# Moving tiles at drawn positions modulo 256 bytes in a two-layer decoder trunk

## The chip, the cores and the metric

One core of one Trainium2 chip runs the kernel. The metric is the device time in microseconds of one execution, as the median of several runs.

## The reference

Two layers on 256 tokens of width 2048, fp32. Each layer has a token mixer and then a gated network with a causal convolution of width 3; each of these four parts is preceded by an RMS norm with a shift and scale that come from a conditioning vector, and followed by a gate. Cut to what matters here:

```python
def stick_breaking_mixer(h, qkv_w, o_w):
    ...
    o = stick_breaking_attention(qkv[0], qkv[1], qkv[2])
    o = o.transpose(0, 2, 1, 3).reshape(bsz, t_len, d)
    return o @ o_w                              # 2048 -> 2048

def conv_ffn(h, up_w, dw_w, dw_b, down_w):
    u = causal_depthwise_conv(h @ up_w, dw_w, dw_b)      # 2048 -> 2 x 5632
    gt, val = jnp.split(u, 2, axis=-1)
    return (jax.nn.silu(gt) * val) @ down_w              # 5632 -> 2048

# layer 0: convolution module, conv_ffn; layer 1: stick_breaking_mixer, conv_ffn; final norm
x = x + gate * y
x = x + gate * conv_ffn(h, ffn_up_w[i], ffn_dw_w[i], ffn_dw_b[i], ffn_down_w[i])
```

## The kernel before

Everything is held transposed: a tile has 128 features on the partitions and the 256 tokens along the row. A product of two fp32 matrices is made of three matmuls in the type fp32r, since each operand is split into a high part (rounded) and a low part (the rest). The weights are the stationary operand, `wh` and `wl`; the activations are the moving operand, a pair of tiles of 256 columns. The function `gemm` writes them at lines 298 to 300 of the kernel (L298: high weights by high activations; L299: high weights by low activations; L300: low weights by high activations).

The moving pairs are:

- `hh`, `hl`: the normed input of a part, 16 pairs. They feed the first products of the networks ("up") and the products for queries and keys. They are not touched.
- `gh`, `gl`: the gated values between the two products of a network. A network's 44 tiles of 128 features go in two halves of 22; each half is made by an up product (`up_done` splits it into a pair) and consumed by a second product ("down"), which adds 22 tiles into each of the 16 output blocks. There are 23 buffers for the pairs, gh0 to gh22, so the second half begins with gh22, then gh0, gh1 and so on. The pool of network 0 is called g0, of network 1 g1.
- `oh`, `ol`: the results of the 16 attention heads, which feed the product "o".
- `zh`, `zl`: the output of the convolution module's norm, which feeds "pw2". Not touched.

The order of the matmuls comes from `plan`: the first four output blocks of a second product or of o take turns, tile by tile (four triples of matmuls on one moving pair, then the next pair); for the last four tiles, and for all the later blocks, one block runs over all its tiles. Down in halves is therefore 16 x 22 x 3 = 1056 matmuls, four such stages in the program; o is 16 x 16 x 3 = 768.

Weights arrive by DMA from SP's queue in pieces of 128 x 1024 (`raw`), ACT rounds them to `wh` (L244), and DVE makes `wl` (L248). During the network of layer 0, the rows for the later shifts, scales and gates come by DMA from POOL's queue into a ring of tiles `mraw` (three in one pool, two in a pool "mods" opened behind g0), and DVE reduces each (L331), in order between its other work.

Where a tile lies in its row of SBUF follows from the order in which a pool hands out tiles. The helper `skewed` allocates each of the z, g and o tiles 8 floats longer than its 256, so that the next tile begins 1056 bytes on, which is 32 bytes further modulo 256. The first tile of g0, of g1 and of o begins at 160 modulo 256:

```python
SKEW = {"z": (1, 1), "g0": (1, 1), "g1": (1, 1), "o": (1, 1)}
...
return pool.tile([P, T + 8 * SKEW[kind][low]], F32R, name=name)[:, :T]
...
gh[j] = skewed(gpool, f"g{i}", 0, f"gh{j % NG}")
gl[j] = skewed(gpool, f"g{i}", 1, f"gl{j % NG}")
```

High and low tiles alternate, so gh0, gl0, gh1, gl1 lie at 160, 192, 224, 0 and so on. The `hh` and `hl` tiles (258 floats, laid out in steps of 1056 bytes) have the same even steps.

Of the kernel before, what the change touches and what calls it, by code (L numbers as in the profile page):

```python
# [11 lines left out]
F32R = mybir.dt.float32r  # L12
# [4 lines left out]
P = 128  # L17
# [7 lines left out]
LATE_POOL, LATE_PE = 10, 8  # L25
PRODUCTS = 11

SKEW = {"z": (1, 1), "g0": (1, 1), "g1": (1, 1), "o": (1, 1)}
HEAD = 16
UBUFS = 9  # L30
M0 = 6
# [86 lines left out]
def hybrid_trunk(ctx: ExitStack, tc: tile.TileContext, cfg: Cfg, io: dict):  # L118
    nc = tc.nc
    D, T, H = cfg.D, cfg.T, cfg.H  # L120
# [115 lines left out]
    def split_next(later=False):  # L236

        blocks, v, n = raws[len(parts)]
        if stream[len(parts)][0] == "pw1":
            parts.append((blocks, v, None))  # L240
            return
        wh = w_pool.tile([P, PW], F32R, name="wh")
        wl = w_pool.tile([P, PW], F32R, name="wl")
        nc.scalar.copy(wh[:, :n], v[:, :n])  # L244
        parts.append((blocks, wh, wl))

        def low():
            nc.vector.tensor_tensor(wl[:, :n], v[:, :n], wh[:, :n].bitcast(F32), op=ALU.subtract)  # L248

        if later:  # L250
            return low
        low()
# [117 lines left out]

    def skewed(pool, kind, low, name):

        return pool.tile([P, T + 8 * SKEW[kind][low]], F32R, name=name)[:, :T]

    def split_act(t, hh, hl, bias=None):

# [119 lines left out]
    with ExitStack() as cv:  # L496
# [321 lines left out]
        for c in range(KD + 1):  # L818
# [6 lines left out]
            if c > 0:  # L825
                old = [(c - 1, k) for k in vector_taps(c - 1)[split(c - 1):]]
                n = max(len(taps), len(old))
                pad = lambda v: v + [None] * (n - len(v))
                taps = [t for pair in zip(pad(taps), pad(old)) for t in pair if t]
            made = 0  # L830
            for s in range(nd):
# [10 lines left out]
                if c == 0 and s % 2 == 1 and 2 + s // 2 < NH:  # L842
                    j = 2 + s // 2
# [5 lines left out]
                if c == KD and s == 0:  # L849
                    low = split_next(later=True)  # L850
# [68 lines left out]
        for j in range(KD + 1):  # L919
            if j < KD:  # L920
                zt.append(t256())
                if j > 1:
                    nc.vector.tensor_tensor(ys[j], ys[j], dm, op=ALU.subtract)
                nc.vector.tensor_tensor(zt[j], ys[j], rs, op=ALU.mult)
                nc.scalar.activation(zt[j], zt[j], AF.Silu, bias=pc("ln_b", j, 1), scale=pc("ln_g", j, 1))
            if j == 1:
                low()
            if j > 0:
                zs.append([skewed(zpool, "z", n == "zl", f"{n}{j - 1}") for n in ("zh", "zl")])
                split_act(zt[j - 1], *zs[j - 1])  # L930
            if j in (1, 2, 4):
                split_next()
# [18 lines left out]
    def ffn(i, entry, out):  # L951
        m = f"ffn{i}"
        NG = KF // 2 + 1
        with ExitStack() as fs:
# [16 lines left out]
            def up_done(nb, ps):  # L971
                pend[nb] = conv3(ps, nb)
                j = nb % KF
                if not (j in pend and j + KF in pend):
                    return
                yg, yv = pend.pop(j), pend.pop(j + KF)
                s = t256()
                nc.scalar.activation(s, yg, AF.Silu)
                nc.vector.tensor_tensor(s, s, yv, op=ALU.mult)
                gh[j] = skewed(gpool, f"g{i}", 0, f"gh{j % NG}")  # L980
                gl[j] = skewed(gpool, f"g{i}", 1, f"gl{j % NG}")
                nc.scalar.copy(gh[j], s)
                nc.vector.tensor_tensor(gl[j], s, gh[j].bitcast(F32), op=ALU.subtract)
# [57 lines left out]
    with ExitStack() as at:  # L1041
# [100 lines left out]
        for g in range(H // GH):  # L1142
            if g == 0:
                hh, hl = entry1.product("qk0a", qk_done, "natural_log_exp_and_others")
# [161 lines left out]
```

## Time and profile before

| | |
|---|---|
| median of 3 runs (range) | 2307.48 us (2307.41 to 2308.37) |
| span of the profiled execution, first to last instruction | 2304.7 us (the page gives no other time of it) |
| PE busy | 2270.8 us, 99% |
| DVE, ACT, POOL busy | 75%, 51%, 15% |
| HBM read | 598.58 MB, 261 GB/s over the span |
| granted TensorE clock, mean | 0.997 of full speed |

PE is TensorE's matmuls, PEld its weight loads, DVE VectorE, ACT ScalarE, POOL GpSimd, SP the engine whose queue issues most DMAs. The matmuls of one stream overlap: a matmul's own duration is longer than the distance from its start to the start of the next, and it is the distance that adds up. "PEclk" is the granted clock as a share of full speed (in tenths in the page's row of 40 slices).

In the profile the stages that use the touched tiles lie at: down of network 0, 668.0 to 792.1 us and 1027.4 to 1155.3; o, 1455.2 to 1547.8; down of network 1, 1808.2 to 1932.2 and 2167.6 to 2291.4.

### The profile page before, as it was taken

The page shows a single profiled execution, that of the slowest core. Times are in us where ns is not written, and L with a number is a line of the kernel's source. Part 1 is how long each engine was busy: PE and PEld are TensorE (multiplying, and loading weights), DVE is VectorE, ACT ScalarE, POOL GpSimd, SP SyncE. Part 2 cuts the span into 40 slices and gives each one's busy share as a digit, 9 for nine tenths or more (in the row PEclk, how much of TensorE's full clock was granted, in tenths as well). Part 3 has the DMA queues.
Part 4 walks back from the last instruction along what each step waited for, and adds up shares of the span by engine and source line. Part 5 has one row for each costly group of instructions (what it writes and reads, how often), then busy time and mean ns, then how long its engine had stood idle before and what let it go on. Part 6 is the DMA issues. An engine that isn't in the chain of part 4 may idle for free.

```text
span 2304.7 us, 44243 instructions
## 1 busy us (share of the span) xinstructions
PE 2270.8 (99%) x17834; PEld 2168.1 (94%) x17834; DVE 1736.7 (75%) x2386; ACT 1164.4 (51%) x1776; POOL 334.6 (15%) x478
## 2 busy tenths in 40 slices
PE   7999999999999999999999999999999999999997
PEld 5888678999999999999999999999999999999997
DVE  7689968899998899999975555668666545666654
ACT  2056655755543355554465555657555434555443
POOL 4058713200000000002111000121000000000010
PEclk9999999999999999999999999999999999999999
DMA  9988799789999999999854555555555555555553
GB/s 397 417 328 306 272 368 355 272 320 356 358 347 384 363 345 361 355 350 345 304 189 159 165 173 167 172 190 179 190 187 189 187 188 186 190 189 187 190 185 110
DMA packets 139167, 603.56 MB, mean 262 GB/s; under 512 B 15441, under 2 KB 15569, under 8 KB 115153
## 3 DMA queue, kind: packets, MB, share of 16 engines
q1 hardware_dynamic: 120242, 464.42, 56.0%
q0 software_dynamic: 18720, 136.32, 15.8%
q8 instruction: 139, 2.28, 0.4%
q14 instruction: 66, 0.54, 0.1%
HBM read 598.58 MB, written 2.10 MB: 261 GB/s over the span
## 4 chain that ended last, share of the span: by engine, by line
PE 88%; DVE 5%; DMA 4%; ACT 1%; issue 1%; POOL 0%; DVEq 0%; SPq 0%; POOLq 0%; ACTq 0%
PE ps L298 25%; PE ps L299 25%; PE ps L300 25%; PE ps L664 5%; DMA mraw<-in_mt_mix 3%; DVE mraw L331 2%; DVE wl L248 1%; PE ps L1133 1%; PE ps L1131 1%; PE ps L1132 1%; DMA mraw<-in_mt_ffn 1%; PE ps L577 1%; PE auxa L577 1%; DVE hl L382 0%; PE auxb L1132 0%
## 5 line engine op out<-in xcount | busy, mean ns | idle before, releaser
L248 DVE TENSOR_TENSOR wl<-raw,wh 128x1024 fp32r<-128x1024 f32 x688 | 842.9, 1229 | 412.7 <-ACT wh L244 408.0
L244 ACT CAST wh<-raw 128x1024 fp32r<-128x1024 f32 x688 | 719.5, 1048 | 823.9 <-PE ps L299 642.1
L298 PE MATMUL ps<-hh,wh 128*128 128x256 f32 (+1 forms) x3264 | 915.8, 281 | 0.0
L299 PE MATMUL ps<-hl,wh 128*128 128x256 f32 (+1 forms) x3264 | 912.1, 279 | 0.0
L300 PE MATMUL ps<-hh,wl 128*128 128x256 f32 (+1 forms) x3264 | 908.3, 278 | 0.1
L299 PEld LDWEIGHTS ps<-hl,wh 128*128 128x128 f32 x3264 | 617.7, 189 | 0.3
L300 PEld LDWEIGHTS ps<-hh,wl 128*128 128x128 f32 x3264 | 612.8, 188 | 0.7 <-DVE wl L248 0.7
L298 PEld LDWEIGHTS ps<-hh,wh 128*128 128x128 f32 x3264 | 612.7, 188 | 0.3
L299 PE MATMUL ps<-gl,wh 128*128 128x256 f32 x1408 | 396.0, 281 | 0.0
L300 PE MATMUL ps<-gh,wl 128*128 128x256 f32 x1408 | 393.7, 280 | 2.1 <-DVE wl L248 2.1
L298 PE MATMUL ps<-gh,wh 128*128 128x256 f32 x1408 | 394.9, 280 | 0.0
L331 DVE CUSTOM_DVE_ANT_0 mraw<-mraw,csr 128x2048 f32<-128x2048 f32 x152 | 348.2, 2292 | 46.3 <-DMA mraw<-in_mt_mix 30.2
L300 PEld LDWEIGHTS ps<-gh,wl 128*128 128x128 f32 x1408 | 265.5, 189 | 2.3 <-DVE wl L248 2.3
L299 PEld LDWEIGHTS ps<-gl,wh 128*128 128x128 f32 x1408 | 266.5, 189 | 0.0
L298 PEld LDWEIGHTS ps<-gh,wh 128*128 128x128 f32 x1408 | 265.6, 189 | 0.0
L397 POOL TENSOR_TENSOR sumsq<-sumsq,t 128x256 f32<-128x256 f32 x56 | 66.2, 1183 | 879.8 <-ACT t L393 879.5
L664 PE MATMUL ps<-hh,raw 128*128 128x256 f32 x832 | 188.8, 382 | 0.0
L664 PEld LDWEIGHTS ps<-hh,raw 128*128 128x128 f32 x832 | 157.8, 191 | 28.3 <-issue 5.8
L967 DVE SCALAR_TENSOR_TENSOR t<-ps,par,t 128x254 f32<-128x254 f32 x328 | 157.3, 480 | 3.9
L704 DVE SCALAR_TENSOR_TENSOR auxb<-u,cpar,auxb 128x256 f32<-128x256 f32 x297 | 121.6, 483 | 4.5 <-ACT auxb L688 3.7
L839 POOL TENSOR_TENSOR y<-y,hl 128x256 f32<-128x256 f32 x143 | 104.4, 730 | 13.4 <-ACT hl L713 3.3
L964 ACT ACTIVATE t<-ps,par 128x256 f32<-128x256 f32 x164 | 91.9, 560 | 0.0
(247 smaller groups left out, 2270.5 us busy)
## 6 DMA issues: line engine op xcount, KB each, us to landing
raw<-in_w_down SPq DMA_DIRECT2D x176, 512.0 KB, 4.5
mraw<-in_mt_ffn POOLq DMA_DIRECT2D x64, 1024.0 KB, 8.3
raw<-in_w_pw SPq DMA_DIRECT2D x96, 512.0 KB, 8.0
mraw<-in_mt_mix POOLq DMA_DIRECT2D x48, 1024.0 KB, 8.2
raw<-in_w_up01b SPq DMA_DIRECT2D x84, 512.0 KB, 7.0
raw<-in_w_up11b SPq DMA_DIRECT2D x84, 512.0 KB, 3.5
raw<-in_w_up00b SPq DMA_DIRECT2D x80, 512.0 KB, 7.6
raw<-in_w_up10b SPq DMA_DIRECT2D x80, 512.0 KB, 3.5
```

The source lines that it names most:

```text
L244: nc.scalar.copy(wh[:, :n], v[:, :n])
L248: nc.vector.tensor_tensor(wl[:, :n], v[:, :n], wh[:, :n].bitcast(F32), op=ALU.subtract)
L298: nc.tensor.matmul(o, wh[:, c], xh[kt], start=first, stop=False, skip_group_check=halves > 0)
L299: nc.tensor.matmul(o, wh[:, c], xl[kt], start=False, stop=False, skip_group_check=halves > 0)
L300: nc.tensor.matmul(o, wl[:, c], xh[kt], start=False, stop=left[nb] == 0, skip_group_check=halves > 0)
L331: nc.vector.tensor_tensor_reduce(out=v, in0=v, in1=csr, scale=1.0, scalar=0.0, op0=ALU.mult, op1=ALU.add, accum_out=macc[:, nb:nb + 1])
L397: engine.tensor_tensor(self.sum, self.sum, sq, op=ALU.add)
L664: nc.tensor.matmul(banks[j][:, nb // KD * T:(nb // KD + 1) * T], w[:, b * P:(b + 1) * P], hf[kt], start=first, stop=left[j] == 0, skip_gro ...
L704: nc.vector.scalar_tensor_tensor(conv_ps[j], us[j % UBUFS][:, k:k + T], tap(j, k), conv_ps[j], op0=ALU.mult, op1=ALU.add)
L839: nc.gpsimd.tensor_tensor(ys[c], ys[c], pr, op=ALU.add)
L964: nc.scalar.activation(y, ps[:, :T], AF.Identity, bias=pc(f"fdb{i}", nb, 1), scale=w(FW - 1))
L967: nc.vector.scalar_tensor_tensor(y[:, s:], ps[:, :T - s], w(k), y[:, s:], op0=ALU.mult, op1=ALU.add)
```

## The change

The even steps of g0, g1 and o are replaced by a table. For each name a position modulo 256 bytes, in steps of 32, is taken from a shuffled list of the 64 pairs (position of the high tile, position of the low tile), with a fixed seed for each pool; the tiles are padded in front and behind so that they land there. In g1 every position has 16 bytes more (the argument `half`). z keeps its even steps. Nothing else changes: the same instructions stand in the same order on every engine.

```diff
-SKEW = {"z": (1, 1), "g0": (1, 1), "g1": (1, 1), "o": (1, 1)}
+def phases(names, base, half, seed):
+
+    rng = np.random.default_rng(seed)
+    n = len(names) // 2
+    pairs = [(a, b) for a in range(8) for b in range(8)]
+    rng.shuffle(pairs)
+    want = [p for pair in pairs[:n] for p in pair]
+    out, at = {}, base
+    for i, name in enumerate(names):
+        pad = (want[i] - at // 32) % 8 if i == 0 else 0
+        nxt = 0 if i + 1 == len(names) else (want[i + 1] - (at // 32 + pad + 32 + half)) % 8
+        size = (pad + 32 + half + nxt) * 8
+        out[name] = (pad * 8 + 4 * half, size)
+        at += size * 4
+    return out
+
+
+G_NAMES = [f"g{x}{j}" for j in range(23) for x in "hl"]
+O_NAMES = [f"o{x}{j}" for j in range(16) for x in "hl"]
+PHASES = {"g0": phases(G_NAMES, 160, 0, 1), "g1": phases(G_NAMES, 160, 1, 2), "o": phases(O_NAMES, 160, 0, 3)}
...
     def skewed(pool, kind, low, name):
 
-        return pool.tile([P, T + 8 * SKEW[kind][low]], F32R, name=name)[:, :T]
+        if kind == "z":
+            return pool.tile([P, T + 8], F32R, name=name)[:, :T]
+        at, n = PHASES[kind][name]
+        return pool.tile([P, n], F32R, name=name)[:, at:at + T]
```

The positions that come out, in units of 32 bytes modulo 256, for the first pairs (high, low): before, in all three pools, (5,6) (7,0) (1,2) (3,4) (5,6) (7,0); after, g0 (7,5) (3,0) (4,5) (3,1) (7,2) (3,6); g1 (5.5,6.5) (3.5,3.5) (3.5,4.5) (3.5,1.5) (7.5,1.5) (5.5,4.5); o (5,4) (0,0) (0,4) (0,2) (3,7) (0,3).

## The prediction

> **What bounds the kernel now.** I read the page first: the busy time by engine, and the chain of work that ended last by line.
>
> ```profile
> span 2304.7 us, 44243 instructions
> PE 2270.8 (99%) x17834; PEld 2168.1 (94%) x17834; DVE 1736.7 (75%) x2386; ACT 1164.4 (51%) x1776; POOL 334.6 (15%) x478
> PEclk9999999999999999999999999999999999999999
> PE 88%; DVE 5%; DMA 4%; ACT 1%; issue 1%; POOL 0%; DVEq 0%; SPq 0%; POOLq 0%; ACTq 0%
> ```
>
> TensorE is busy for 99% of the span at its full granted clock, and 88% of the chain is PE. A nanosecond more per matmul is a nanosecond more of span wherever PE never waits. Next come the groups of PE by form; the change touches the rows with gh, gl, oh and ol.
>
> ```profile
> L298 PE MATMUL ps<-hh,wh 128*128 128x256 f32 x3072 | 861.0, 280 | 0.0
> L299 PE MATMUL ps<-hl,wh 128*128 128x256 f32 x3072 | 857.8, 279 | 0.0
> L300 PE MATMUL ps<-hh,wl 128*128 128x256 f32 x3072 | 853.8, 278 | 0.0
> L299 PE MATMUL ps<-gl,wh 128*128 128x256 f32 x1408 | 396.0, 281 | 0.0
> L298 PE MATMUL ps<-gh,wh 128*128 128x256 f32 x1408 | 394.9, 280 | 0.0
> L300 PE MATMUL ps<-gh,wl 128*128 128x256 f32 x1408 | 393.7, 280 | 2.1 <-DVE wl L248 2.1
> L298 PE MATMUL ps<-oh,wh 128*128 128x256 f32 x256 | 71.8, 281 | 0.0
> L299 PE MATMUL ps<-ol,wh 128*128 128x256 f32 x256 | 71.6, 280 | 0.0
> L300 PE MATMUL ps<-oh,wl 128*128 128x256 f32 x256 | 71.2, 278 | 0.0
> ```
>
> So 4224 matmuls read gh and gl, and 768 read oh and ol: 4992 whose moving address moves. The durations overlap, so they are no cost. The cost is the distance from one start to the next, which I take from stretches of known count: one output block over 22 moving tiles is 66 matmuls, over 16 tiles 48. (A stretch's x also counts the two or three matmuls that overlap its ends, so I use the plan's count.)
>
> ```profile
> core 0: us, PE busy (x), PEclk, DMA share, GB/s
> 668.03:693.57 25.54, 25.54 (x219) 1.00 0.96 369
> 699.18:703.08 3.90, 3.90 (x36) 1.00 1.03 385
> 703.08:706.93 3.85, 3.85 (x35) 1.00 0.99 388
> 803.42:809.02 5.60, 5.60 (x51) 1.00 0.80 309
> 1560.31:1568.96 8.65, 8.65 (x75) 1.00 0.20 61
> 1480.72:1542.32 61.60, 61.60 (x531) 1.00 0.58 189
> ```
>
> PE never idles in these and the clock is full, yet the pace differs:
> - 803.42 to 809.02, one block of the up product over the 16 hh/hl pairs: 5.60 us / 48 = 116.67 ns. Along the tiles the position climbs evenly (hh, hl 32 B on, back to hh, next hh 64 B on), and 16 steps of 64 B close the circle of 256 B, so the pattern never breaks.
> - 1480.72 to 1542.32, eleven blocks over the 16 oh/ol pairs, with the same steps: 61.60 / 528 = 116.67 ns.
> - 699.18 to 703.08, the first 33 matmuls of a block of the second product: 3.90 / 33 = 118.2 ns. Its 22 tiles end at position 224 (gh21) and begin again at 160 (gh0), a jump that breaks the pattern.
> - 703.08 to 706.93, the other 33 of the same block: 3.85 / 33 = 116.7 ns, back at the even pace.
> - 668.03 to 693.57, the opening of that product, where four blocks take turns so that a tile is read four times before the next: 25.54 / 216 = 118.2 ns.
> - 1560.31 to 1568.96, the 258-wide form of the up product, four blocks in turn: 8.65 / 72 = 120.1 ns; less two columns at 116.67/256 each it is 119.2 ns.
>
> DMA traffic does not set this: it is as high in the slow half as in the fast half of one block (385 and 388 GB/s). I read it so: the order of positions modulo 256 B sets the pace, an even order runs at 116.67 ns, and one break costs about 47 ns over the next 33 matmuls before the even pace returns.
>
> **The change part by part.** No instruction is added, removed or moved: on every engine and queue, SP's and POOL's too, the same instructions stand in the same order with the same waits. What differs is addresses. Writes of gh, gl, oh, ol by ACT and DVE keep their size; both engines have slack (51% and 75%). The pools grow by some 4 KB, which shifts the two extra ring tiles of the modulation rows and the attention's small tiles; the nearest rows for a matmul at other positions give at most 3 ns (120.1 against 116.67), and fewer than 300 attention matmuls make that under 1 us either way: taken as nothing.
>
> The matmuls are the term. In the drawn order hardly a step is the old one: gh0, gl0, gh1, gl1, gh2, gl2 lie at 224, 160, 96, 0, 128, 160 bytes modulo 256 in the first network. The pattern is broken at every tile and does not get its 33 matmuls to settle. The lower end for a matmul is the even pace, 116.67 ns; the upper end is 119.2 ns (the disturbed 258-wide form). The nearest rows are the 118.2 ns behind one break and in the opening; as breaks now follow each other without pause I go a little above, to 118.6 ns. The stages as they stand:
>
> ```profile
> 668.03:792.10 124.07, 124.07 (x1057) 1.00 0.98 378
> 1027.42:1155.27 127.85, 125.71 (x1057) 0.99 0.86 322
> 1808.16:1932.23 124.07, 124.07 (x1057) 1.00 0.57 187
> 2167.55:2291.44 123.89, 123.89 (x1057) 1.00 0.47 154
> ```
>
> Each has 1056 matmuls: 1056 x 118.6 = 125.24 us. Against 124.07 that is +1.17 us, twice; against 123.89, +1.35, twice (the second stage, with its stall taken out, is built like the fourth). Together +5.0 us. The heads' product has 576 matmuls behind its opening, from 116.67 to 118.6 ns: +1.1 us, and its opening of 192 at about 118.2 adds 0.1. Sum +6.2 us.
>
> One cover takes something back. In the second stage PE stalls, and the chain there shows why:
>
> ```profile
> 1050.98 2.20 DVE mraw L331
> ...
> 1088.66 7.93 DMA mraw<-in_mt_ffn
> 1096.65 2.18 issue
> ...
> 1100.49 0.38 PE ps L300
> ```
>
> Between 1051 and 1100.5 us the end is set by the modulation rows (a load that DVE waits for, in order, ahead of the weights' low parts), not by PE. Some 400 matmuls lie in there, and 1.2 ns more on each, 0.5 us, vanishes in the stall. How the stall is built:
>
> ```profile
> DVE mraw L331 <- DMA mraw<-in_mt_ffn: 5.5, 2, 5.2
> PE ps L300 <- DVE wl L248: 2.1, 1, 2.1
> 1101.00:1105.00 4.00, 4.00 (x23) 0.57 0.85 309
> ```
>
> PE waits 2.1 us, and then runs four microseconds at a granted clock of 0.57, which costs 1.7 more. If the shorter wait kept the clock up, 1.7 us would come back; if the load landed later, the same could be lost. The wait would still be 1.6 us, near the 2.1 that we see, so I take nothing. The stall goes on being set by DVE and DMA; nothing new becomes late elsewhere, since every engine that feeds PE gets more time.
>
> Sum: +6.2 - 0.5 = +5.7 us. The profiled span of 2304.7 becomes 2310.4. The page gives no time of its own beside the span; the median of the timed runs, 2307.48, lies 2.8 above it, so I forecast 2313.2 us, +0.25%. Below 0.2% (4.6 us) this measurement can't tell a change from none.
>
> [...]
>
> **The rivals.**
> - No change that can be told. The pace has only two levels in these rows, and drawn steps may be as often good as bad: DVE, clock and width all equal, a block now averages 7.75/66 = 117.4 ns, half disturbed and half not. If drawn positions average the same 117.4, the networks give 0 and the heads' product 576 x 0.75 = +0.4 us; at 118.2 it is +3.4 + 0.9 - 0.3. That gives 2307.5 to 2311.5 us. For it: 118.2 is what two of the disturbed rows show. Against: those rows still have even stretches in them.
> - Faster. What decides is the pace of the drawn order: to be told from no change it must be below 116.5 ns (4.6 us / 4992 = 0.92 ns under the present mean of 117.4). At 116.2 ns the stages lose 1.36 us twice and 1.18 twice, the heads' product 0.3: -5.4 us, 2302.1 us. For it: each block now loses 47 ns to its break, and a drawn order might happen not to fall behind. Against: no stretch that I read runs below 116.67 ns over a whole block.
> - Slower by more, through the second network's start at an odd 16 bytes: its tiles would touch a piece more at the end. The row nearest is the 258-wide form, 8 bytes past a full tile: 120.14 - 116.67 = 3.5 ns, of which two columns are 0.9. The other 2.6 ns on 2112 matmuls is 5.4 us on top: 2318.6 us. Against: part of the 2.6 belongs to the taking of turns.
>
> **How the numbers follow.** Forecast (about 118.6 ns) 0.45; odd 16 bytes 0.13, slower too; no change that can be told 0.34; faster 0.08. Slower is therefore 0.58, same 0.34, faster 0.08. The ends of the matmul term give 2304.4 (all at 116.67: -0.87 twice, -0.69 twice) and 2316.2 us (all at 119.2); with the odd 16 bytes 2318.6. The range leaves out the part under 2308 and over 2319 us.
>
> **What would show it.** In the profile after: the stretch of one block of the second product (66 matmuls) at about 7.83 us instead of 7.75, with no fast second half; a stage of 1056 at 125.2 us; the up products' blocks still at 5.60 us; a block of the heads' product at 5.69 instead of 5.60. If the second network's stages are longer than the first's by more than 1 us, the odd 16 bytes cost. I am wrong if the blocks stand at 7.75 us or below, or if the stall near 1100 us changes by more than the matmuls do.

## The result and the profile after

The changed kernel takes 2312.48 us (median of 18 runs), the kernel before beside it 2308.12 us: +4.4 us, ratio 1.0019 with a 95% interval of 1.0012 to 1.0026. The interval is clear of 1, so it is slower, by a little less than the 0.2% (4.6 us) that the prediction named as the least that can be told from no change.

The first lines of the page after:

```profile
span 2309.9 us, 44243 instructions
PE 2275.9 (99%) x17834; PEld 2173.0 (94%) x17834; DVE 1736.5 (75%) x2386; ACT 1164.9 (50%) x1776; POOL 333.3 (14%) x478
PE 87%; DVE 6%; DMA 4%; issue 1%; ACT 1%; POOL 0%; DVEq 0%; SPq 0%; POOLq 0%; ACTq 0%
```

The span is 5.2 us longer and PE's busy time 5.1 us longer; DVE and ACT work as long as before (1736.7 and 1164.4 us). The longer part is TensorE itself. The groups of PE by form show which matmuls (columns: count, busy us, mean ns of one, idle before):

```profile
L317 PE MATMUL ps<-hh,wh 128*128 128x256 f32 x3072 | 861.0, 280 | 0.0
...
L317 PE MATMUL ps<-gh,wh 128*128 128x256 f32 x1408 | 396.3, 281 | 0.0
L319 PE MATMUL ps<-gh,wl 128*128 128x256 f32 x1408 | 396.1, 281 | 2.3 <-DVE wl L267 2.2
L318 PE MATMUL ps<-gl,wh 128*128 128x256 f32 x1408 | 395.6, 281 | 0.0
...
L317 PE MATMUL ps<-oh,wh 128*128 128x256 f32 x256 | 72.3, 283 | 0.0
```

The hh group is the same to the tenth (861.0 us). The two gh groups and the oh group grew, the gl group did not (396.0 before): these are sums of durations that overlap (280 ns each where starts lie 118 ns apart), so they only point at the place. The distance between starts is again read from stretches of known count. First the kernel before, ten whole blocks of the second product of network 0 (660 matmuls), of o (480), and of the two halves of network 1 (660 each):

```profile
core 0: us, PE busy (x), PEclk, DMA share, GB/s
706.93:784.47 77.54, 77.54 (x663) 1.00 0.99 379
1486.32:1542.32 56.00, 56.00 (x483) 1.00 0.58 189
1847.06:1924.60 77.54, 77.54 (x663) 1.00 0.58 186
2206.41:2283.81 77.40, 77.40 (x662) 1.00 0.46 152
```

and the changed kernel, with ten blocks of the up product (480) ahead of them:

```profile
810.01:866.01 56.00, 56.00 (x482) 1.00 0.91 342
707.41:785.41 78.00, 78.00 (x662) 1.00 0.99 373
1488.70:1545.56 56.86, 56.86 (x482) 1.00 0.55 186
1850.57:1928.77 78.20, 78.20 (x662) 1.00 0.54 183
2210.89:2288.96 78.07, 78.07 (x663) 1.00 0.44 150
```

The untouched up product stands at 56.00 / 480 = 116.67 ns, as before. Network 0 goes from 117.5 to 78.00 / 660 = 118.18 ns, o from 116.67 to 56.86 / 480 = 118.46, network 1 from 117.5 and 117.3 to 118.48 and 118.29 ns. The clock is full and PE never idle in all of them. The fast second half of a block is gone: by the start times in the trace, averaged over eleven blocks of network 0, the first 33 matmuls of a block start 118.0 ns apart and the other 33 118.4 (before, 118.2 and 116.8). The whole stages after:

```profile
668.40:793.10 124.70, 124.70 (x1058) 1.00 0.99 376
1028.41:1157.36 128.95, 126.61 (x1057) 0.99 0.85 319
1457.42:1551.13 93.71, 93.71 (x789) 1.00 0.54 180
1811.49:1936.47 124.98, 124.98 (x1057) 1.00 0.56 186
2171.81:2296.64 124.83, 124.83 (x1057) 1.00 0.45 152
```

```profile
1455.21:1547.80 92.59, 92.59 (x789) 1.00 0.56 183
```

Against the prediction's rows of before, and this one for o, the five stages are longer by 0.63, 1.10, 1.12, 0.91 and 0.94 us: 4.7 of the 5.2 us. Another 0.4 lies ahead of 668 us, where no touched tile has been read (the stage begins at 668.40 instead of 668.03). In the experiments that leave the weights in place it begins anywhere from 668.2 us (e7) to 669.5 (e10), so this part is not put down to the change.

### The profile page after: what moved, and what is told of

Its sections match the earlier page's. It is cut to its first block, busy times and chain, and to the rows that moved or that the text cites. A ratio compares the mean times of both kernels' runs of the same rounds, so it can differ in the third digit from the quotient of the medians.

```text
span 2309.9 us, 44243 instructions
## 1 busy us (share of the span) xinstructions
PE 2275.9 (99%) x17834; PEld 2173.0 (94%) x17834; DVE 1736.5 (75%) x2386; ACT 1164.9 (50%) x1776; POOL 333.3 (14%) x478
## 4 chain that ended last, share of the span: by engine, by line
PE 87%; DVE 6%; DMA 4%; issue 1%; ACT 1%; POOL 0%; DVEq 0%; SPq 0%; POOLq 0%; ACTq 0%
PE ps L317 25%; PE ps L318 25%; PE ps L319 25%; PE ps L686 5%; DMA mraw<-in_mt_mix 3%; DVE mraw L350 2%; DMA mraw<-in_mt_ffn 1%; DVE wl L267 1%; PE ps L1153 1%; PE ps L1155 1%; PE ps L1154 1%; PE ps L599 1%; PE auxa L599 1%; DVE hl L404 0%; PE auxb L1154 0%
## 5 line engine op out<-in xcount | busy, mean ns | idle before, releaser
L419 POOL TENSOR_TENSOR sumsq<-sumsq,t 128x256 f32<-128x256 f32 x56 | 64.8, 1158 | 886.2 <-ACT t L415 886.0
```

Source lines behind the costliest of these rows:

```text
L419: engine.tensor_tensor(self.sum, self.sum, sq, op=ALU.add)
```

## The experiments

The question was what in a position costs time. The theory of the prediction, "breaks": any even order of positions settles at 116.67 ns, and what costs is a break in it. Rivals: each order has a pace of its own; the odd 16 bytes of the second network; and what is not an order of the moving tiles at all, their position against the weights, which all lie at 32 modulo 256. (Positions are worked out from the order of allocation; the profile shows no addresses.) All kernels use one helper in place of the table, and differ in the wanted positions (units of 32 bytes):

```diff
+def placed(names, base, want):
+    out, at = {}, base
+    for name, w in zip(names, want):
+        pad = int(w * 32 - at) % 256
+        size = -(-(pad + 1024) // 32) * 32
+        out[name] = (pad // 4, size // 4)
+        at += size
+    return out
+def even(n, first, low, step):
+    return [(first + step * j + i * low) % 8 for j in range(n) for i in range(2)]
+def drawn(n, seed, half=0):
+    pairs = [(a, b) for a in range(8) for b in range(8)]
+    np.random.default_rng(seed).shuffle(pairs)
+    return [p + half / 2 for pair in pairs[:n] for p in pair]
```

`even(23, 5, 1, 2)` is the order of the kernel before; `drawn` gives the draws of the change, 16 bytes further on where `half` is 1. The edits are put in short: "PLACES: g0 X" stands for `"g0": placed(G_NAMES, 160, X)`. Rows below are ten blocks each, as above, where nothing else is said. All but e9 and e10 ran once each, so only their windows are compared, not their times.

**Constant position, shifted order, pairs at one position** (e1).

```diff
+PLACES: g0 even(23, 5, 0, 0); g1 even(23, 5.5, 1, 2); o even(16, 5, 0, 2)
```

> Three even orders, one in each pool: g0 with every tile at the same position (160 modulo 256), g1 with the old even steps but 16 bytes further on, o with high and low tile of a pair at the same position and 64 B from pair to pair. Read: one block of the second product (66 matmuls) in g0 and g1, one block of o (48). Theory 'breaks' (any even order that closes settles at 116.67 ns; only breaks cost): g0 7.70 us (no break at all), g1 7.74 to 7.75 as in the kernel before (the odd 16 bytes cost nothing), o 5.60. Rival 'own steps' (each step from one position to the next has its own price, whatever came before): g0 differs from 7.70 by more than 0.03, as every one of its steps is a step of 0; o differs from 5.60. Rival 'odd 16 bytes': g1 7.82 or more.

Windows of e1: g0, o, and g1 in its first half.

```profile
707.55:785.87 78.32, 78.32 (x662) 1.00 0.99 377
1488.50:1545.30 56.80, 56.80 (x482) 1.00 0.57 187
1850.09:1927.82 77.73, 77.73 (x662) 1.00 0.57 185
```

The theory of breaks falls at once: g0 has no break, and runs at 118.67 ns, slower than the drawn order. o, also without a break, is at 118.33. The even order 16 bytes further on loses 0.19 us in ten blocks against 77.54: less than its rival asked, but more than the 7.74 to 7.75 us a block that "breaks" allowed.

**Other draws, and the 16 bytes alone** (e2).

```diff
+PLACES: g0 drawn(23, 4); g1 drawn(23, 2); o drawn(16, 3, 1)
```

> Other draws: g0 from another seed; g1 with the draw of the changed kernel but without the odd 16 bytes; o with the draw of the changed kernel plus 16 bytes. Theory 'breaks': every draw stands at 118.2 to 118.5 ns, so g0 7.80 to 7.82 us for 66 matmuls, and 16 bytes do nothing: g1 7.82 as in the changed kernel, o 5.69 as there. Rival 'odd 16 bytes': g1 falls to 7.80 or below (it was 118.48 ns with them against 118.18 for g0 without), o rises above 5.70. If each step has its own price, g0 of another seed may lie anywhere from 7.70 to 7.90.

Windows of e2: g0, o, g1.

```profile
707.51:785.58 78.07, 78.07 (x662) 1.00 0.98 376
1486.38:1542.98 56.60, 56.60 (x482) 1.00 0.58 187
1847.92:1926.12 78.20, 78.20 (x663) 1.00 0.58 184
```

Another draw stands at 118.29 ns, beside 118.18. The draw of network 1 takes 78.20 us with the odd 16 bytes and without; that of o becomes faster with them (56.60 against 56.86). So no surcharge of the 16 bytes shows in these two draws.

**Breaks counted** (e3).

```diff
+PLACES: g0 even(23, 5, 1, 4)
+g1: [(p + 2 * (j > 9) + 2 * (j > 31)) % 8 for j, p in enumerate(even(23, 5, 1, 2))]
+o:  [(p + 2 * (j > 15)) % 8 for j, p in enumerate(even(16, 5, 1, 2))]
```

> Breaks counted. g0: from pair to pair 128 B instead of 64 (high, then low 32 B on), which closes over 22 pairs: no break. g1: 64 B steps with two steps of 128 B at the tenth and twenty-first further pair, which closes over 22 pairs: two small breaks instead of the one large. o: the old steps with one step of 128 B in the middle and, where the block ends, one of 0: two breaks. Theory 'breaks': g0 7.70 us, g1 between 7.74 and 7.78, o about 5.60 + 2 x 24 x 1.3 ns = 5.66. Rival 'own steps': g0 off 7.70 by more than 0.03; g1 and o within 0.02 of 7.70 and 5.60, since only two steps in 66 or 48 differ.

```profile
707.57:786.04 78.47, 78.47 (x663) 1.00 0.97 375
1488.14:1544.54 56.40, 56.40 (x482) 1.00 0.58 188
1849.34:1926.54 77.20, 77.20 (x662) 1.00 0.57 187
```

In g1 the two steps of 128 B stand before gh5 and gh16, and not at the pairs that the expectation names, since the index counts tiles; there are two of them, and the order closes, all the same. g0 (first row) has no break and is the slowest yet, 118.9 ns. Where the order is the old one, breaks do cost, as expected in kind: two in each block of o make 117.5 ns out of 116.67. In g1 the two smaller breaks cost less than the old large one (77.20 against 77.54). So a break cost time where the order without it stands at 116.67 ns; e9 below has breaks that cost none.

**The drawn orders, rotated** (e4).

```diff
+PLACES: g0 [p + 1 for p in drawn(23, 1)]; g1 [p + 2 for p in drawn(23, 2, 1)]; o [p + 4 for p in drawn(16, 3)]
```

> The draws of the changed kernel, each pool rotated as a whole: g0 by 32 B, g1 by 64 B, o by 128 B; every step from tile to tile stays, only the place relative to 256 B and to the weights (all at 32 modulo 256) changes. Theory 'steps of the moving tiles alone' : blocks equal to the changed kernel's within 0.005 us: 7.800, 7.820 (second halves 7.787, 7.807), 5.687. Rival 'against the weights or absolute places': blocks differ by more than 0.01 us, in either direction.

Windows of e4: g0 and g1; then two single blocks of o, one after the other; then five blocks (330 matmuls) ahead of PE's wait in the second half of network 0, and five behind it.

```profile
708.38:786.51 78.13, 78.13 (x662) 1.00 0.98 375
1850.83:1928.56 77.73, 77.73 (x662) 1.00 0.58 185
```

```profile
1489.15:1494.87 5.72, 5.72 (x51) 1.00 0.57 187
1494.87:1500.52 5.65, 5.65 (x50) 1.00 0.56 186
1060.79:1099.66 38.87, 38.87 (x333) 1.00 0.90 336
1111.10:1150.13 39.03, 39.03 (x333) 1.00 0.84 317
```

With every step between moving tiles kept, network 1 goes from 78.20 to 77.73 us and network 0 from 78.00 to 78.13. The ten blocks of o still take 56.87 together, but they now alternate between about 5.72 and 5.65 us, where the changed kernel had 5.69 in each. The steps alone don't set the pace. Nor do the positions alone: the last two rows have the same tiles in the same order, at 117.8 ns ahead of the wait and 118.3 behind it. Why was not looked into.

**The weights moved, the moving tiles left** (e5). Each weight buffer is 32 bytes longer, so that the eight lie at eight positions.

```diff
-MORE_ROWS = 4
+MORE_ROWS = 3
...
-        wh = w_pool.tile([P, PW], F32R, name="wh")
-        wl = w_pool.tile([P, PW], F32R, name="wl")
+        wh = w_pool.tile([P, PW + 8], F32R, name="wh")[:, :PW]
+        wl = w_pool.tile([P, PW + 8], F32R, name="wl")[:, :PW]
...
```

> The kernel before with its moving tiles where they were, and the weights moved instead: the eight wh and wl buffers lie at 32, 64, ... 256 B modulo 256 in place of all at 32 (one buffer fewer for the rows of the first modulation makes the room, so the time up to about 285 us is not compared). Theory 'moving against the weights': blocks of the up product (48 matmuls, 5.60 us before), of the second product (7.753, 7.740) and of o (5.60) leave their values by more than 0.02 us and differ from one weight buffer to the next. Rival 'steps of the moving tiles alone': all three stay to 0.005 us.

Windows of e5: up product and o.

```profile
813.80:870.37 56.57, 56.57 (x483) 1.00 0.90 339
1493.94:1550.61 56.67, 56.67 (x483) 1.00 0.56 187
```

Both stood at 56.00. The second product of network 0 goes from 77.54 to 77.90, and its blocks no longer agree (7.76 to 7.82 us, all 7.75 before). Not a moving tile lies elsewhere modulo 256; only the weights do.

**Constant positions at several distances from the weights** (e6).

```diff
+PLACES: g0 even(23, 1, 0, 0); g1 even(23, 3, 0, 0); o even(16, 0, 0, 0)
```

> Every tile of a pool at one position, as g0 in the first experiment (160 modulo 256, 7.832 us per 66 matmuls, 118.7 ns): now g0 at 32, which is where the weights lie, g1 at 96, o at 0. Steps are 0 everywhere. 'Steps of the moving tiles alone': 7.83 in g0 and in g1, 5.69 to 5.70 in o, whatever the position. 'Moving against the weights': the three differ from 118.7 ns by more than 0.3 ns, and g0 most.

```profile
708.18:787.38 79.20, 79.20 (x662) 1.00 0.98 372
1491.61:1548.41 56.80, 56.80 (x482) 1.00 0.59 186
1853.19:1930.92 77.73, 77.73 (x662) 1.00 0.58 185
```

At the weights' own position 79.20 / 660 = 120.00 ns, the slowest of all; 64 bytes after it (third row) 117.77; 32 bytes before it (second) 118.33; and 128 bytes from it, in e1, 118.67.

**Position or distance** (e11). All weights move by 128 bytes together, by an empty tile ahead of them; the moving tiles are constant again.

```diff
-MORE_ROWS = 4
+MORE_ROWS = 3
...
+    w_pool.tile([P, 32], F32, name="gap", bufs=1)
...
+PLACES: g0 even(23, 1, 0, 0); g1 even(23, 5, 0, 0); o even(16, 4, 0, 0)
```

> All weights moved together by 128 B, to 160 modulo 256 (one buffer fewer for the rows of the first modulation makes the room, so the time up to about 285 us is not compared), and constant positions for the moving tiles: g0 at 32, g1 at 160, o at 128. Theory 'the distance from the weights counts': g1, now at the weights' position, stands at 120.00 ns (7.920 us), where it was g0 at 32 with the weights at 32; g0, 128 B from the weights, at 118.7 ns (7.832), as it was at 160 with the weights at 32; o, 32 B before the weights, at 118.3 (5.680). Rival 'the place itself counts': g0 at 32 stays at 7.920 and g1 at 160 at 7.832.

Windows of e11: g0, o, g1.

```profile
708.72:787.04 78.32, 78.32 (x662) 1.00 0.99 374
1489.11:1545.91 56.80, 56.80 (x482) 1.00 0.58 187
1851.45:1930.65 79.20, 79.20 (x662) 1.00 0.56 182
```

g0 at 32, which cost 79.20 with the weights there, now takes the 78.32 of the distance 128; g1 at 160, where e1's g0 had 78.32, now takes 79.20. For the constant positions that ran, the pace went with the distance between the moving tile and the weights (78.32 twice at 128 bytes, 79.20 twice at 0, and 56.80 twice for o, 32 bytes before them), not with the place. That it counts modulo 256 bytes was not tested by itself, since e11 brings back whole distances. One order of e8 (below) speaks for it: in network 1 each pair lies 2304 bytes, nine times 256, behind the last, and each tile's three matmuls take the same time, 352.5 to 353.8 ns on average over eleven blocks of the trace.

**Six more even orders** (e7, e8).

```diff
+e7: g0 even(23, 5, 3, 4); g1 even(23, 5, 2, 4); o even(16, 5, 2, 2)
+e8: g0 even(23, 5, 4, 4); g1 even(23, 5, 1, 0); o even(16, 5, 7, 2)
```

> Three other even orders without a break: g0 (low tile 96 B behind its high tile, next pair 128 B on), g1 (64 B, 128 B), o (64 B, 64 B). If any even order that closes were to settle at 116.67 ns, 7.70, 7.70 and 5.60; the first and third experiment say no (118.3 to 118.9 ns). What I expect now, 'each order has a pace of its own, and the old one is a good one': 7.78 to 7.87, 7.78 to 7.87, 5.64 to 5.72, with none under 116.67 ns.

> Three more even orders: g0 (low tile 128 B behind its high tile, next pair 128 B on), g1 (32 B, next pair at the same position), o (low tile 32 B before its high tile, next pair 64 B on). Expected as in the one before: 7.78 to 7.87, 7.78 to 7.87, 5.64 to 5.72. If only the size of a step counted and not its sign, o would stand at 5.60.

Windows of e7: g0, o, g1.

```profile
706.94:783.94 77.00, 77.00 (x662) 1.00 0.99 382
1485.84:1541.84 56.00, 56.00 (x483) 1.00 0.57 189
1846.82:1924.92 78.10, 78.10 (x663) 1.00 0.55 184
```

Two of the three stand at 116.67 ns, which I had not expected, the third at 118.3. e8 gave 118.7, 117.8 and 117.2 ns (78.37, 77.74 and 56.27 us); the last two are a little faster than expected, and o is not at 56.00, so the sign of a step counted too. The even orders without a break that ran, constant ones among them, lie between 116.67 and 120.00 ns, and none below.

**The best and the worst order, timed** (e9, e10).

```diff
+e9:  g0 and g1 even(23, 5, 3, 4); o even(16, 5, 1, 2)
+e10: g0 and g1 even(23, 1, 0, 0); o even(16, 1, 0, 0)
```

> g0 and g1 in the order that stood at 116.67 ns in the seventh experiment (low tile 96 B behind its high tile, next pair 128 B on), o as in the kernel before. Theory 'positions against the weights set the pace, and nothing else changes': blocks 7.700 us in all four stages, stages of 123.4 us, against 124.07, 123.9, 124.07 and 123.89 before: 0.6 + 0.5 + 0.6 + 0.5 = 2.2 us less by the stages without their stall, so a ratio of about 0.9990. Rival 'the second network differs from the first': g1 off 7.70 by more than 0.02.

> Every tile of g0, g1 and o at 32 modulo 256, the position of the weights, which stood at exactly 120.00 ns in the sixth experiment. Theory as above: blocks of 7.920 and 5.760 us, stages of 126.7 us, so 2.65 + 2.8 + 2.65 + 2.85 us more in the networks and 12 x 0.16 + 0.3 us in o: +13.1 us, ratio about 1.0057. Rival 'the pace of TensorE is partly hidden behind the loads of the weights': less than +10 us.

e9 takes 2305.41 us against 2308.32, ratio 0.9988 (0.9980 to 0.9997); e10 2319.30 us, ratio 1.0048 (1.0034 to 1.0061). Windows of e9 (g0, g1, and the second half of g1), then of e10 (g0, o):

```profile
707.57:784.57 77.00, 77.00 (x662) 1.00 0.99 382
1847.17:1924.17 77.00, 77.00 (x662) 1.00 0.55 186
2205.79:2282.79 77.00, 77.00 (x663) 1.00 0.45 152
```

```profile
709.13:788.33 79.20, 79.20 (x662) 1.00 0.98 372
1492.13:1549.73 57.60, 57.60 (x482) 1.00 0.55 184
```

The blocks are as expected: in e10 ten blocks take 79.20 us in both halves of network 1 as well, though the DMA engines are busy for 0.53 and 0.44 of the time there and for 0.98 in the row above. The times agree: +11.0 us where I had +13.1 (interval +7.8 to +14.1), -2.9 where I had -2.2 (-4.6 to -0.7). The interval of e10 alone would leave its rival, less than +10 us, open; the blocks decide against it. Some of what is missing lies in e10's second stage, which grew by 1.6 us and not 2.8: no wait there is longer than 0.8 us, and the granted clock over ten blocks of it is 1.00. e9 beats both kernels, by 0.12% against the kernel before.

The third row of e9 says more about breaks. In a second half the tiles begin with gh22, then gh0, and in this order gh20, gh22 and gh0 lie at one position: twice in each block a step of 0 stands where the order has 128 bytes. It cost nothing: 77.00, as in the rows above it.

## Why the prediction was right, and where its steps failed

- **The pace of the drawn order.** I took 118.6 ns; it is 118.2 in network 0 and 118.3 to 118.5 in network 1 and o. That term of +6.2 us came out at +4.7 over the five stages. It was the lower of the disturbed rows that fitted, not a little above it.
- **The cover at 1050 to 1100 us.** I let 0.5 us vanish there, since a chain of loads and not PE was to set the end of the wait. It did not vanish: the second stage grew by 1.10 us, by more than the first (0.63), and PE's idle time in it went from 2.14 to 2.34 us (the stage less PE's busy time in its row). Counted from the start of the stage, the wait ended at 73.07 us before (1100.49) and at 73.87 after (1102.28): the chain moved along with PE. The clock behind the wait is as before; these rows are of the changed kernel, the wait and a window right behind it:

```profile
PE ps L319 <- DVE wl L267: 2.2, 1, 2.2
1103.00:1107.00 4.00, 4.00 (x24) 0.57 0.92 317
```

  The prediction counted 1.7 us for a clock that would stay up behind a shorter wait. In e2 the second stage has two short waits (1.1 us the longest) and a granted clock of 1.00, and is 2.2 us longer than the first stage (124.85, with the window's end set alike) instead of 4.25:

```profile
PE ps L325 <- DVE wl L273: 1.7, 2, 1.1
1028.64:1155.65 127.01, 125.32 (x1058) 1.00 0.86 324
```

  All thirteen kernels agree: over ten blocks of this stage the mean granted clock is 0.98 where one wait of PE lasts 1.9 us or more (before, after, e4, e6, e7, e9), and 1.00 where the longest is 1.8 us or less (the other seven). The prediction reckoned with a wait of 1.6 us and took nothing for the clock; had the wait come down to that, the 1.7 us would, by an estimate from these runs, have come back. It did no harm only because the wait did not shrink. Why the wait is split in some kernels was not tried.
- **Outside the span, and the sum.** I added 2.8 us, the distance of the median from the profiled span; after, it is 2.6 (2312.48 against 2309.9). The profiled execution itself took 1.8 us more than its span (2311.74), so of the 2.8 about 1 us is, by estimate, that the profiled execution of before was faster than its median; that would also explain why the span grew by 5.2 us and the median by 4.4. The forecast of 2313.2 was 0.7 us too high: -1.5 in the pace and -0.2 here, +0.5 for the cover that did not come and +0.5 outside the five stages. Errors of both signs cancelled in part, and that is luck.
- **The mechanism.** The prediction read the slow first half of a block as a break in an even order and called every unbroken order 116.67 ns. The second half of that step is wrong. An order without a break can be slower than the drawn one (e1 118.67, e3 118.9, e6 120.00 ns, against 118.2 to 118.5), and the pace changed with where the moving tile lies against the weights (e5: o from 56.00 to 56.67 us; e6 and e11: 79.20 and 78.32 us for one position). That the number held is luck in good part: the nine drawn orders that ran stand at 117.8 to 118.5 ns, near the disturbed rows' 118.2, and the prediction had no reason for it that lasted. Why draws land near the middle of 116.67 to 120.00 ns was not tested.
- **The rival without change.** Its mechanism, that the drawn order averages to the present pace, is refuted: every drawn order that ran, three in the changed kernel, three in e2 and three in e4, stands above the pace it replaced. Its upper end is not refuted: with 118.2 ns it had +4.0 us, nearer to the measured +4.4 than the forecast's +5.7.
- **The odd 16 bytes.** Refuted as a surcharge by e2 (78.20 us with them and without). That such a tile touches a piece more at its end was the author's supposition, which no run shows. The even order shifted by 16 bytes (e1, 77.73 against 77.54) shows that a place 16 bytes on can change the pace all the same.

What stays open is the mechanism. The runs show that the distance from the weights counts (e6 and e11, 79.20 against 78.32 us), that the order counts with it (e7, e8, 116.67 to 118.7 ns), and that one order can hold two paces (e4, 117.8 and 118.3 ns). None of them shows why, and nothing here says in advance which order is at 116.67 ns.

## What to carry to other kernels

In this kernel, whose TensorE is busy for 99% of the span and reads fp32r tiles back to back, 3.3 ns in 117 lie between the best and the worst order that was timed (e9, e10), or 14 us of 2308. In a kernel like it, the positions of the moving tiles modulo 256 bytes, and the weights', are worth choosing on purpose and measuring. Measure an order by blocks of known count in a window of the profile, several of them since they need not agree; that resolves what a time of the whole kernel hardly does. A rule read from two halves of one block can give the right size for the wrong reason, so change the other operand too before believing it.

## What the runs showed of the hardware

Many settled paces lie on one grid, as far as rows of 0.01 us show it. Ten blocks take 77.00, 77.20, 77.40, 77.54, 78.00, 78.07, 78.20 or 79.20 us, and 56.00, 56.40, 56.60, 56.80, 56.86 or 57.60: worked out from these, one block is a whole multiple of 6.667 ns (1155, 1158, 1161, 1163, 1170, 1171, 1173, 1188, and 840, 846, 849, 852, 853, 864 of them). Other orders repeat only over several blocks: o in e4 over two, the constant order of e1 (78.32) over five. I had expected a pace that could lie anywhere.

None of the orders, draws and distances went under 116.67 ns for 256 columns over whole blocks, though single matmuls start closer to each other: by the start times in the trace, the distances in e9 go round 119, 118, 112, 119, 120, 112 ns, which is 116.67 on average. At the weights' own position (e6) every distance in a settled block is 120 ns.
